# Wider column blocks for the queries and gates of a two-layer encoder: 512 columns and two token tiles to a buffer

## The chip, the cores and the metric

One core of a Trainium2 chip runs the whole program in one launch. The metric is device microseconds, first instruction to last and what lies around it, lower is better; the kernel's time is the median of several executions. The profile shown is one execution taken by the hardware profiler. The core has a matmul engine (PE, with its weight loads PEld), a vector engine (DVE), a scalar engine (ACT), a general engine (POOL) and SP, which here issues all transfers. Each takes its own instructions strictly in the order in which they were written into the program.

## The reference, cut to what matters

Two layers over 2048 tokens of 1024 features. The first is a state-space scan beside a convolution module and is untouched here. The second is sparse attention:

```
proj = rms_norm(h) @ w_in        # 1024 -> 1024 q, 1024 z, 256 k, 256 v, 512 qi, 64 ki, 8 wi
q, k, qi, ki get a partial rotary (the first 16 of each 64 columns)
score[t, s] = sum over 8 index heads of wi[t, h] * relu(qi[t, h] . ki[s])
idx = the 256 best admissible keys of each token
out = softmax(q . k[idx] / 8) @ v[idx]            # 16 heads, 4 of them on one key head
y = (out * silu(z)) @ w_out;  h + y;  final norm
```

## The kernel before, in words

Token tiles are 128 rows, 16 of them; a half is 8 tiles. In the second layer the normalised activations of one half lie transposed in SBUF, as a high and a low part (`hb`), and every projection is made of three matmuls (high by high, low by high, high by low) for each of 8 feature tiles, so that a block of columns over 8 token tiles takes 8 x 8 x 3 = 192 matmuls. `token_major` runs a block in groups of two token tiles, with three PSUM buffers (`ps_tm`); the stationary operand is a tile of `hb`, the moving one a row tile of the weights (`wh` high, `wl` low).

`load_w` fetches a block's weights in pieces of 128 x 512 numbers: a transfer into one of two staging buffers (`wst`, L106), a rounding copy on ACT (`wh`, L113) and a subtraction on POOL (`wl`, L114). There are eight buffers each for `wh` and `wl`. A block of 256 columns fills four of them, so that two blocks fit side by side.

`project_half` goes through a list of blocks. Its inner function `done` copies each finished token tile from PSUM to `ot` (two buffers; by a plain copy, or by SiLU for the gates), and when `ot` is full `finish` rotates what needs it on POOL (`rope_`, six operations) and stores it.

The order of the second layer is: both halves' index blocks (`first`), the index scores and the selection of the 256 best keys for tiles 2 to 15 (`index`), then the remaining blocks of half 1, a swap of `hb`, the remaining blocks of half 0 (`rest`: k, v, four blocks of q, four of z per half), and attention. A scheduler then merges these: it places instructions by program order as priority and by its own timeline, and what it writes is fixed for every engine. So the projections of `rest` stand between the instructions of the index work.

Index scoring goes by chunks of up to 512 keys: for each of 8 heads two matmuls into `ps_i`, a `relu` on ACT (L913) and a multiply-add on DVE (L72, into `sc` or, for the last four tiles, `scl`, which is stored to `sc_d`). There are 38 chunks; tiles 14 and 15 have the last eight. Selection (`select_mask`) searches a threshold bit by bit, 34 counting passes a tile: on DVE (L977) with two small steps on POOL (L69) behind each, or, for the odd tiles up to 13, on ACT (L994, L1002, L1004). Selection of tiles 12 to 15 is a second, late part (`late`): its first 140 steps, nearly all of tile 12, are written ahead of attention, and the rest is spread over attention by columns. Attention (`Attend`) has `ps_s` matmuls, a masked maximum on DVE (`lm`, L1121), an exponential on ACT, transposes (`ps_pt`) and values (`ps_pv`).

Of the kernel before, what the change touches and what calls it, by code (L numbers as in the profile page):

```python
# [11 lines left out]
F32 = mybir.dt.float32  # L12
# [11 lines left out]
P = 128  # L24
# [346 lines left out]
def norm_to_feature(k, tiles, layer, hT, col0, vec, ident, sm, ev, pt, split=False, parts=1):  # L371


    nc = k.nc
    n = len(tiles)
    ss = sm.tile([P, parts, n], F32, tag="ss", name="ss")
    rs = sm.tile([P, n], F32, tag="rs", name="rs")
    w = D // parts
    for i, xt in enumerate(tiles):
        junk = ev.tile([P, w], BF16, tag="junk", name="junk", bufs=1)  # L380
        for a in range(parts):
            x, acc = xt[:, a * w:a * w + w], ss[:, a, i:i + 1]
            if split and i % 2:
                nc.vector.tensor_tensor_reduce(out=junk, in0=x, in1=x, scale=1.0, scalar=0.0, op0=ALU.mult,
                                               op1=ALU.add, accum_out=acc)
            else:
                nc.scalar.activation(junk, x, AF.Square, accum_out=acc)
    for a in range(1, parts):
        k.vtt(ss[:, 0], ss[:, 0], ss[:, a], ALU.add)
    ss = ss[:, 0]  # L390
    k.vts(ss, ss, 1.0 / D, ALU.mult, EPS, ALU.add)
    k.rsqrt(rs, ss, sm, "rsq")
    for i, xt in enumerate(tiles):
        if split and i % 2:
            nc.scalar.activation(xt, xt, AF.Copy, scale=rs[:, i:i + 1])
        else:
            k.vts(xt, xt, rs[:, i:i + 1], ALU.mult)
    cols = slice(col0, col0 + n * P)
    for f in range(NF):
        ps = pt.tile([P, n, 128], F32, tag="pt", name="ps_t")  # L400
        for i, xt in enumerate(tiles):
            nc.tensor.transpose(ps[:, i], xt[:, f * P:(f + 1) * P], ident)
        g = vec[:, VEC_NG + layer * 8 + f:VEC_NG + layer * 8 + f + 1]
        hi, lo = hT[f]
        psf = ps.rearrange("p a b -> p (a b)")
        nc.scalar.activation(hi[:, cols], psf, AF.Copy, scale=g)
        k.stt(lo[:, cols], psf, g, hi[:, cols].bitcast(F32), ALU.mult, ALU.subtract)
# [7 lines left out]
def token_major(k, pj, act, W, ncol, tiles, done, group=4):  # L415


    for g in range(0, len(tiles), group):
        grp = tiles[g:g + group]
        pss = [pj.tile([P, 512], F32, tag="pj", name="ps_tm") for _ in grp]  # L420
        for f in range(NF):
            for ps, i in zip(pss, grp):
                c = slice(i * P, i * P + P)
                k.mm3(ps[:, 0:ncol], (act[f][0][:, c], act[f][1][:, c]), W[f], f == 0, f == NF - 1)
        for ps, i in zip(pss, grp):
            done(i, ps[:, 0:ncol])
# [309 lines left out]
OQ, OZ, OK, OV, OQI, OKI = 0, 1024, 2048, 2304, 2560, 3072  # L736
# [17 lines left out]
def split2(k, v, hi2, lo2):  # L754

    nc = k.nc
    for a in range(2):
        nc.scalar.copy(hi2[:, :, :, a], v)
    for a in range(2):
        nc.gpsimd.tensor_tensor(out=lo2[:, :, :, a], in0=v, in1=hi2[:, :, :, 0].bitcast(F32), op=ALU.subtract)  # L760
# [17 lines left out]
def project_half(k, h, hT, new, order, A, h1_d, S, st, rope, ident, identr, vec, pools):  # L778


    nc = k.nc
    hp, xp, ev, op, wp, sm, pj, pt = pools
    w1 = A["w_in1"]

    def rope_(t, t0, nh):

        v = t.rearrange("p t (h c) -> p t h c", c=64)
        X, Y = v[:, :, :, 0:8], v[:, :, :, 8:16]
        sh = [P, 4, nh, 8]
        c = rope[:, t0:t0 + 4, None, 0:8].to_broadcast(sh)  # L790
        s = rope[:, t0:t0 + 4, None, 8:16].to_broadcast(sh)
        r = sm.tile([P, 2, 4, 4, 8], F32, tag="ropet", name="ropet", bufs=1)
        r = r[:, :, :, 0:nh]
        g = nc.gpsimd
        k.vtt(r[:, 0], Y, s, ALU.mult, g)
        k.vtt(r[:, 1], X, s, ALU.mult, g)
        k.vtt(X, X, c, ALU.mult, g)
        k.vtt(Y, Y, c, ALU.mult, g)
        k.vtt(X, X, r[:, 0], ALU.subtract, g)
        k.vtt(Y, Y, r[:, 1], ALU.add, g)  # L800

    def both_parts(v, name):

        kd = ev.tile([P, 4, 1, 2, 64], F32R, tag="kd", name=name)
        kl = ev.tile([P, 4, 1, 2, 64], F32R, tag="kdl", name=name + "l", bufs=1)
        split2(k, v, kd, kl)
        return kd, kl

    def doubled(src, out):

        ps = pt.tile([P, 4, 128], F32R, tag="pt", name="ps_k")
        for i in range(4):
            nc.tensor.transpose(ps[:, i], src[:, i, 0].rearrange("p a b -> p (a b)"), identr)
        nc.scalar.copy(out, ps.rearrange("p a b -> p (a b)"))

    def index_key(kt, t0, rows):
        rope_(kt[:, :, 0:64], t0, 1)
        k.vts(st["wi"][:, t0:t0 + 4], kt[:, :, 64:72], float(np.float32(8 ** -0.5)), ALU.mult,
              0.125, ALU.mult, eng=nc.gpsimd)
        kd, kl = both_parts(kt[:, :, None, 0:64], "kid")  # L820
        for src, dst in ((kd, "kih"), (kl, "kil")):
            doubled(src, st[dst][:, rows])

    def stack_k(ot, rows):

        for kv in range(4):
            v = ot[:, :, None, kv * 64:kv * 64 + 64]
            kd, kl = both_parts(v, "kd")
            for src, dst in ((kd, S["kh"][kv]), (kl, S["kl"][kv])):
                ks = ev.tile([P, 512], F32R, tag="ks", name="ks", bufs=1)  # L830
                doubled(src, ks)
                nc.sync.dma_start(dst[:, rows], ks.bitcast(F32))

    for grp in range(4 if new else 0):
        with k.tc.high_priority(offset=1500):
            tiles = []
            for i in range(2):
                xt = xp.tile([P, D], F32, tag="xt", name="xt1")
                r0 = h * HALF + (grp * 2 + i) * P
                nc.sync.dma_start(xt, h1_d[r0:r0 + P])  # L840
                tiles.append(xt)
            norm_to_feature(k, tiles, 1, hT, grp * 256, vec, ident, sm, ev, pt, parts=2)

    def finish(c, ot, t0):

        rows = slice(t0 * P, t0 * P + 512)
        if c < OZ or OK <= c < OV or c >= OQI:
            rope_(ot, t0, 4)
        if c == OK:
            stack_k(ot, rows)  # L850
            return
        if c < OZ:
            dst = S["q"][rows, c:c + 256]
        elif c < OK:
            dst = S["z"][rows, c - OZ:c - OZ + 256]
        elif c == OV:
            dst = S["v"][rows]
        else:
            dst = S["qi"][rows, c - OQI:c - OQI + 256]
        nc.sync.dma_start(dst.rearrange("(t p) c -> p t c", p=P), ot)  # L860

    for c0, ncol in order:
        W = k.load_w(w1, 0, NF, c0, ncol, wp)
        cur = {}

        def done(j, ps):
            g, ji = divmod(j, 4)
            if ji == 0:
                cur["ot"] = op.tile([P, 4, 256], F32, tag="ot", name="ot")
                if ncol == 328:  # L870
                    cur["kt"] = ev.tile([P, 4, 72], F32, tag="ks", name="kit", bufs=1)
            if OZ <= c0 < OK:
                nc.scalar.activation(cur["ot"][:, ji], ps, AF.Silu)
            else:
                nc.scalar.copy(cur["ot"][:, ji], ps[:, 0:256])  # L875
            if ncol == 328:
                nc.scalar.copy(cur["kt"][:, ji], ps[:, 256:328])
            if ji == 3:
                t0 = h * 8 + g * 4
                finish(c0, cur["ot"], t0)  # L880
                if ncol == 328:
                    index_key(cur["kt"], t0, slice(t0 * P, t0 * P + 512))

        token_major(k, pj, hT, W, ncol, list(range(8)), done, 2)
# [303 lines left out]
def layer1(k, A, h1_d, S, ident, identr, vec):  # L1188
    nc, tc = k.nc, k.tc
    with ExitStack() as ctx:  # L1190
# [3 lines left out]
        with ExitStack() as c2:  # L1194
# [4 lines left out]
            wp, ev, sm = tags(junk=1, wh=8, wst=2), {}, tags(ss=2, rs=2, rsqh=2, rsqt=2)  # L1199
# [3 lines left out]
            op = pool(c2, "ot1", 2, side="right")  # L1203
            sm.update(tags(rope=1, ropet=1))
            pools = (hp, xp, Tags(ev), op, Tags(wp), Tags(sm), pool(c2, "pj1", 3, space=PSUM), pt)
            rope = pools[5].tile([P, 16, 16], F32, tag="rope", name="rope")
# [41 lines left out]
            half = lambda h, new, order: project_half(  # L1248
                k, h, hT, new, order, A, h1_d, S, st, rope, ident, identr, vec, pools)
            first = [(OKI - 256, 328), (OQI, 256)]  # L1250
            rest = [(OK, 256), (OV, 256)] + [(c + 256 * i, 256) for c in (OQ, OZ) for i in range(4)]
            half(0, True, first)
            swap_h(True)
            for i in range(2):
# [230 lines left out]
```

## Time and profile before

| what | value |
|---|---|
| median of 3 runs | 3020.63 us (3018.98 to 3023.07) |
| the profiled execution | 3015.91 us, span 3014.1 us |
| PE busy | 2753.4 us (91%), 17488 matmuls |
| DVE busy | 2072.8 us (69%) |
| ACT busy | 1733.2 us (58%) |
| POOL busy | 1105.6 us (37%) |

The profiled execution is 4.7 us below the median of the runs. Shares are averages over stages of very different kinds, so the stage that the change touches, about 1110 to 1790 us of the span, is read by itself. Matmuls are pipelined: what one takes in a stream is the distance of two starts, not the duration shown.

### The profile page before, as it was taken

To read this page: it belongs to the slowest core of one execution; us is meant where nothing else is said; L and a number is where in the kernel's file an instruction comes from. 1 tells how busy PE (TensorE), PEld (TensorE's weight loads), DVE (VectorE), ACT (ScalarE), POOL (GpSimd) and SP (SyncE) were. 2 spreads that over 40 slices of the span, in tenths; PEclk is the share of its full clock that TensorE was granted. 3 is DMA by queue.
4 is the path that set the end of the run, shared out by engine and by line. 5 is a ranking of instruction groups with operands and counts; after the bars stand their busy time and mean duration, and the time that the engine had idled before them with its cause. 6 is when DMAs were issued, how large, how long until landed. Compare 5 with 4: busy or idle time off the path is not lost. (4 is left out here: it accounts for less than half of the span.)

```text
span 3014.1 us, 47682 instructions
## 1 busy us (share of the span) xinstructions
PE 2753.4 (91%) x17488; PEld 2220.8 (74%) x17488; DVE 2072.8 (69%) x3735; ACT 1733.2 (58%) x3558; POOL 1105.6 (37%) x1517
## 2 busy tenths in 40 slices
PE   7789998799999999899889968999989999999998
PEld 5667786678999899899779946666655555666787
DVE  8899986995354556644897479734489997456444
ACT  4122332344243688888768957899965666655311
POOL 3946133732232697745774113321232121001000
PEclk9899999899999999999999979999999999999999
DMA  3254563346566323235322261111110101001332
GB/s 134 76 126 142 157 171 63 122 160 208 172 203 226 97 82 120 64 94 175 99 71 82 88 229 38 58 33 37 38 52 26 47 21 53 22 4 50 123 126 98
DMA packets 233385, 300.40 MB, mean 100 GB/s; under 512 B 14144, under 2 KB 171072, under 8 KB 233024
## 3 DMA queue, kind: packets, MB, share of 16 engines
q1 hardware_dynamic: 233152, 297.37, 31.4%
q8 instruction: 137, 2.24, 0.3%
q14 instruction: 96, 0.79, 0.1%
HBM read 194.16 MB, written 105.25 MB: 99 GB/s over the span
## 5 line engine op out<-in xcount | busy, mean ns | idle before, releaser
L114 POOL TENSOR_TENSOR wl<-wst,wh 128x512 fp32r<-128x512 f32 (+1 forms) x220 | 341.5, 1556 | 444.6 <-ACT wh L113 407.9
L121 PE MATMUL ps_tm<-wh,hb 128*128 128x256 f32 (+1 forms) x1536 | 439.3, 290 | 11.7 <-ACT ot L875 6.9
L122 PE MATMUL ps_tm<-wh,hb 128*128 128x256 f32 (+1 forms) x1536 | 444.4, 290 | 0.8 <-DVE hb L72 0.8
L123 PE MATMUL ps_tm<-wl,hb 128*128 128x256 f32 (+1 forms) x1536 | 439.9, 289 | 0.0
L1132 ACT ACTIVATE lm<-lm,mx 128x512 f32<-128x512 f32 (+15 forms) x256 | 309.1, 1209 | 135.0 <-DVE mx L1121 134.4
L1153 ACT COPY pT<-ps_pt 128x512 f32<-128x512 f32 (+1 forms) x512 | 273.6, 563 | 153.0 <-PE ps_pt L1148 127.0
L72 DVE SCALAR_TENSOR_TENSOR cvo<-hc,vec,cvo 128x1024 f32<-128x1024 f32 x240 | 356.0, 1514 | 0.8
L1121 DVE CUSTOM_DVE_ANT_0 lm<-ps_s,amb 128x1024 f32<-128x1024 f32 (+7 forms) x256 | 249.6, 985 | 152.2 <-PE ps_pt L1148 89.4
L1155 PE MATMUL ps_pv<-pT,v 128*64 128x256 f32 x2176 | 339.1, 399 | 14.6 <-DVE avt L62 8.6
L1148 PEld LDWEIGHTS ps_pt<-ident,lm 128*128 128x128 f32 x2176 | 240.1, 141 | 143.1 <-issue 125.0
L1148 PE MATMUL ps_pt<-ident,lm 128*128 128x128 f32 x2176 | 340.8, 282 | 1.8 <-ACT lm L1132 0.7
L1117 PE MATMUL ps_s<-kh,qs 128*128 128x512 f32 (+2 forms) x640 | 268.6, 421 | 48.7 <-DVE mx L1121 42.1
L121 PEld LDWEIGHTS ps_tm<-wh,hb 128*128 128x128 f32 x1536 | 296.2, 194 | 19.6 <-ACT ot L875 9.0
L69 POOL TENSOR_SCALAR sv<-sv 128x1 f32<-128x1 f32 x512 | 185.6, 363 | 321.6 <-DVE eq L977 282.9
L122 PEld LDWEIGHTS ps_tm<-wh,hb 128*128 128x128 f32 x1536 | 298.0, 194 | 6.0 <-DVE hb L72 1.5
L123 PEld LDWEIGHTS ps_tm<-wl,hb 128*128 128x128 f32 x1536 | 296.7, 194 | 4.3
L113 ACT CAST wh<-wst 128x512 fp32r<-128x512 f32 (+1 forms) x220 | 133.2, 609 | 283.2 <-DMA wst<-in_w_in 131.3
L121 PE MATMUL ps_p<-hh,wh 128*128 128x512 f32 x640 | 256.8, 404 | 18.9 <-ACT uT L520 16.5
L123 PE MATMUL ps_p<-hl,wh 128*128 128x512 f32 x640 | 256.9, 404 | 0.0
L122 PE MATMUL ps_p<-hh,wl 128*128 128x512 f32 x640 | 255.9, 400 | 0.0
L977 DVE TENSOR_SCALAR_CACHE_REDUCE eq<-klo,sv 128x384 bf16<-128x384 uint16 (+7 forms) x136 | 207.0, 1525 | 63.5 <-POOL sv L69 62.8
L977 DVE TENSOR_SCALAR_CACHE_REDUCE eq<-khi,sv 128x384 bf16<-128x384 uint16 (+7 forms) x136 | 206.8, 1525 | 48.7 <-POOL sv L69 47.4
(333 smaller groups left out, 6335.2 us busy)
## 6 DMA issues: line engine op xcount, KB each, us to landing
wst<-in_w_in SPq DMA_DIRECT2D x168, 256.0 KB, 2.9
zs_d<-zt SPq DMA_DIRECT2D x16, 512.0 KB, 3.3
zt<-zs_d SPq DMA_DIRECT2D x16, 512.0 KB, 4.4
ry<-rec_d SPq DMA_DIRECT2D x16, 512.0 KB, 4.2
xr<-in_x SPq DMA_DIRECT2D x16, 512.0 KB, 4.4
wst<-in_w_out SPq DMA_DIRECT2D x32, 256.0 KB, 3.4
h_d<-xr SPq DMA_DIRECT2D x16, 512.0 KB, 3.7
xt<-h_d SPq DMA_DIRECT2D x16, 512.0 KB, 5.7
```

The lines of the kernel that those rows point to most:

```text
L72: self.nc.vector.scalar_tensor_tensor(out=out, in0=a, scalar=s, in1=b, op0=op0, op1=op1)
L114: nc.gpsimd.tensor_tensor(out=lo, in0=st, in1=hi.bitcast(F32), op=ALU.subtract)
L121: t.matmul(ps, a[0], b[0], start=start, stop=False)
L122: t.matmul(ps, a[1], b[0], start=False, stop=False)
L123: t.matmul(ps, a[0], b[1], start=False, stop=stop)
L977: op = nc.vector.tensor_scalar(out=eq, in0=src, scalar1=u, scalar2=0.0, op0=op, op1=ALU.add, accum_out=cnt)
L1117: nc.tensor.matmul(pss[e][:, cols], qs[e][:, 2 * hp + h], src[:, e, cols], start=part == 0, stop=part == 1)
L1121: self.pace[0] = nc.vector.tensor_tensor_reduce(out=prob[e][h][:, c:c + w], in0=pss[e][:, 0:w], in1=mb[:, c:c + w], scale=-0.125, scalar=( ...
L1132: nc.scalar.activation(lm, lm, AF.Exp, bias=mxs[e, h][:, nh - 1:nh], scale=-1.0, accum_out=t["den"][:, hd:hd + 1])
L1148: nc.tensor.transpose(ps[:, s, h], prob[e][h][:, (b + s) * P:(b + s + 1) * P], ident)
L1153: nc.scalar.copy(pT[:, 0:n], ps[:, 0:n].rearrange("p s h q -> p s (h q)"))
L1155: nc.tensor.matmul(po[64 * s:64 * s + 64, e], self.kvt[(b + s) // 8, kp][2][:, (b + s) % 8, e * 64:e * 64 + 64], pT[:, s], start=b == 0, s ...
```

## The change

The blocks of q and z are made 512 columns wide, two a half instead of four. `done` then gathers two token tiles by 512 columns into an `ot` buffer where it gathered four by 256 (the same 512 KB), and `rope_` and `finish` take their sizes from the buffer. The blocks of k, v and the index stay at 256. A weight block of 512 columns fills all eight `wh` and `wl` buffers.

```diff
-        sh = [P, 4, nh, 8]
-        c = rope[:, t0:t0 + 4, None, 0:8].to_broadcast(sh)
-        s = rope[:, t0:t0 + 4, None, 8:16].to_broadcast(sh)
-        r = sm.tile([P, 2, 4, 4, 8], F32, tag="ropet", name="ropet", bufs=1)
+        nt = t.shape[1]
+        sh = [P, nt, nh, 8]
+        c = rope[:, t0:t0 + nt, None, 0:8].to_broadcast(sh)
+        s = rope[:, t0:t0 + nt, None, 8:16].to_broadcast(sh)
+        r = sm.tile([P, 2, nt, 16 // nt, 8], F32, tag="ropet", name="ropet", bufs=1)
...
-        rows = slice(t0 * P, t0 * P + 512)
+        nt, w = ot.shape[1:3]
+        rows = slice(t0 * P, (t0 + nt) * P)
         if c < OZ or OK <= c < OV or c >= OQI:
-            rope_(ot, t0, 4)
+            rope_(ot, t0, w // 64)
...
         def done(j, ps):
-            g, ji = divmod(j, 4)
+            w = 512 if ncol == 512 else 256
+            nt = 1024 // w
+            g, ji = divmod(j, nt)
             if ji == 0:
-                cur["ot"] = op.tile([P, 4, 256], F32, tag="ot", name="ot")
+                cur["ot"] = op.tile([P, nt, w], F32, tag="ot", name="ot")
...
-                nc.scalar.copy(cur["ot"][:, ji], ps[:, 0:256])
+                nc.scalar.copy(cur["ot"][:, ji], ps[:, 0:w])
...
-            if ji == 3:
-                t0 = h * 8 + g * 4
+            if ji == nt - 1:
+                t0 = h * 8 + g * nt
...
-            rest = [(OK, 256), (OV, 256)] + [(c + 256 * i, 256) for c in (OQ, OZ) for i in range(4)]
+            rest = [(OK, 256), (OV, 256)] + [(c + 512 * i, 512) for c in (OQ, OZ) for i in range(2)]
```

The scheduler orders the whole stage anew. Three places matter. The first is ACT from the last copies out of the projections to the first instructions of attention (`ot` are those copies, `relu` is index scoring, `klo` the late selection's keys, `qs` and the table load attention's). Before:

```order
L994 ACTIVATE eq,sv<-klo,sv 128x1536
L873 ACTIVATE ot<-ps_tm 128x256 x2
L913 ACTIVATE relu<-ps_i 128x512 x22
L972 COPY klo<-key 128x512 x3
L972 COPY klo<-key 128x128
```

And in the changed kernel (lines of these helpers are numbered up to four higher):

```order
L998 ACTIVATE eq,sv<-klo,sv 128x1536
L917 ACTIVATE relu<-ps_i 128x512 x3
L877 ACTIVATE ot<-ps_tm 128x512 x2
L917 ACTIVATE relu<-ps_i 128x512 x17
L917 ACTIVATE relu<-ps_i 128x384 x7
...
L917 ACTIVATE relu<-ps_i 128x384
...
L917 ACTIVATE relu<-ps_i 128x512 x2
...
L917 ACTIVATE relu<-ps_i 128x512 x30
```

Behind the last copy out of a projection stood 22 relus of index scoring; now there are 17 + 8 + 2 + 30 = 57.

The second place is DVE at the end of index scoring (`scl` is the multiply-add of a head, `eq` a counting pass of tile 12's late selection, 1664 keys wide, `lm` attention's maximum). Before:

```order
L69 TENSOR_SCALAR scl<-relu,wi 128x512
L72 SCALAR_TENSOR_TENSOR scl<-relu,wi,scl 128x512 x4
...
L971 COPY khi<-key 128x128
L977 TENSOR_SCALAR eq,sv<-khi,sv 128x1664 x3
L1121 ISA lm,mx<-ps_s,amb 128x512
```

And in the changed kernel, at the start of the third chunk from the end (the pattern of the last two rows then goes on to the end of scoring):

```order
L975 COPY khi<-key 128x512
L69 TENSOR_SCALAR key<-scr 128x512
L62 TENSOR_TENSOR key<-key,scr 128x512
L975 COPY khi<-key 128x512
L69 TENSOR_SCALAR key<-scr 128x128
L62 TENSOR_TENSOR key<-key,scr 128x128
L975 COPY khi<-key 128x128
L69 TENSOR_SCALAR scl<-relu,wi 128x512
L981 TENSOR_SCALAR eq,sv<-khi,sv 128x1664
L72 SCALAR_TENSOR_TENSOR scl<-relu,wi,scl 128x512
```

All of tile 12's counting passes stood behind scoring, three of them ahead of the first `lm`; now 23 stand between the multiply-adds of the last three chunks and two more ahead of the first `lm`, so nine of the 34 are left behind it.

The third place is SP's queue around a change of blocks in half 0 (`wst` are weight pieces, `q_d` and `z_d` stores of finished buffers). Before, a stretch of q blocks:

```order
L860 DMA q_d<-ot 128x4x256
L893 DMA qi<-qi_d 128x512
L106 DMA wst<-in_w_in 128x2x256 x3
L860 DMA q_d<-ot 128x4x256
L106 DMA wst<-in_w_in 128x2x256
L931 DMA sc_d<-scl 128x512
L860 DMA q_d<-ot 128x4x256
L106 DMA wst<-in_w_in 128x2x256 x3
```

And in the changed kernel, from the third group of a q block to the first of the next:

```order
L862 DMA q_d<-ot 128x2x512
L106 DMA wst<-in_w_in 128x512 x4
L862 DMA q_d<-ot 128x2x512
L106 DMA wst<-in_w_in 128x512 x2
L935 DMA sc_d<-scl 128x512
L1059 DMA mask_d<-eq 128x1152
L106 DMA wst<-in_w_in 128x512 x2
L862 DMA q_d<-ot 128x2x512
```

Four pieces per 256-column block were spread over the block; now the eight pieces of a block stand together between the stores of the previous block's last groups and the first store of its own.

## Rows read from the trace of the kernel before

**Rows 1.** Span and mean granted TensorE clock.
```profile
core 0: 3014.1 us, clock 0.969
```

**Rows 2.** Busy time by stretch: PE, PEld, DVE, ACT, POOL (instructions), clock, DMA, GB/s.
```profile
1300.00:1350.00 50.00, 49.81 (x395) 49.12 (x395) 22.71 (x51) 40.78 (x112) 16.46 (x22) 0.97 0.31 91
...
1500.00:1550.00 50.00, 43.80 (x310) 40.55 (x308) 47.12 (x65) 36.68 (x81) 39.27 (x68) 0.97 0.24 70
...
1650.00:1700.00 50.00, 50.00 (x389) 48.35 (x388) 30.45 (x41) 47.18 (x104) 13.76 (x10) 1.00 0.33 102
1700.00:1750.00 50.00, 49.87 (x368) 47.51 (x366) 22.73 (x40) 47.03 (x102) 0.74 (x1) 1.00 0.17 56
1750.00:1800.00 50.00, 22.34 (x64) 13.17 (x65) 38.72 (x64) 19.76 (x35) 12.46 (x18) 0.64 0.92 322
```

**Rows 3.** Timeline of PE: start, duration, instruction; last projections, first attention.
```profile
1740.50 0.39 PE L906 MATMUL ps_i<-kih,qis 128*128 128x512 f32 x1
1740.73 0.39 PE L908 MATMUL ps_i<-kil,qis 128*128 128x512 f32 x1
1740.95 0.28 PE L123 MATMUL ps_tm<-wl,hb 128*128 128x256 f32 x1
...
1743.05 0.28 PE L121 MATMUL ps_tm<-wh,hb 128*128 128x256 f32 x1
...
1744.61 0.28 PE L122 MATMUL ps_tm<-wh,hb 128*128 128x256 f32 x1
...
1748.22 0.28 PE L123 MATMUL ps_tm<-wl,hb 128*128 128x256 f32 x1
...
1790.60 0.80 PE L1117 MATMUL ps_s<-kh,qs 128*128 128x512 f32 x1 [4.85 <-ACT qs L774]
```

**Rows 4.** The tile ot: instructions with ns min/median/max.
```profile
L875 ACT COPY ot<-ps_tm x128: 350/370/409, 958.7 to 1627.7; 128x256 f32<-128x256 f32 x128
L873 ACT ACTIVATE ot<-ps_tm x64: 361/383/416, 1299.4 to 1749.6; 128x256 f32<-128x256 f32 x64
L62 POOL TENSOR_TENSOR ropet<-ot,rope x56: 448/460/929, 964.6 to 1629.7; 128x128 f32<-128x128 f32 x56
L860 SPq DMA_DIRECT2D q_d<-ot x16: 359/367/575, 1184.9 to 1633.7; - x16
```

**Rows 5.** Group of relus of 512 columns on ACT: busy us, mean ns, idle before.
```profile
L913 ACT ACTIVATE relu<-ps_i 128x512 f32<-128x512 f32 x208 | 122.7, 599 | 65.1 <-DVE sc L72 21.6 <-DVE scl L72 20.9 <-DVE scl L69 7.0
```

**Rows 6.** Timeline of ACT: tile 14's first relu, the last chunks.
```profile
1681.00 0.58 ACT L913 ACTIVATE relu<-ps_i 128x512 f32<-128x512 f32 x1
1681.48 1.57 ACT L994 ACTIVATE eq<-khi,sv 128x1536 bf16<-128x1536 uint16 x1
1682.95 0.19 ACT L994 ACTIVATION_READ_ACCUMULATOR eq<-khi,sv 128x1 f32 x1
...
1764.65 0.60 ACT L913 ACTIVATE relu<-ps_i 128x512 f32<-128x512 f32 x1 [0.39 <-DVE scl L72]
1765.50 0.60 ACT L913 ACTIVATE relu<-ps_i 128x512 f32<-128x512 f32 x1 [0.26 <-DVE scl L72]
```

**Rows 7.** Timeline of DVE: end of scoring, first counting passes, first lm.
```profile
1776.83 0.49 DVE L69 TENSOR_SCALAR scl<-relu,wi 128x512 f32<-128x512 f32 x1 [7.01 <-DMA sc_d<-scl]
...
1785.19 0.11 DVE L929 MEMSET scl<- 64x64 f32 x1
...
1790.03 1.95 DVE L977 TENSOR_SCALAR_CACHE_REDUCE eq<-khi,sv 128x1664 bf16<-128x1664 uint16 x1
1791.90 0.08 DVE L977 DVE_READ_ACCUMULATOR eq<-khi,sv 128x1 f32 x1
1792.75 1.95 DVE L977 TENSOR_SCALAR_CACHE_REDUCE eq<-khi,sv 128x1664 bf16<-128x1664 uint16 x1 [0.76 <-POOL sv L69]
...
1797.33 0.69 DVE L1121 CUSTOM_DVE_ANT_0 lm<-ps_s,amb 128x512 f32<-128x512 f32 x1
```

**Rows 8.** Weight pieces, 1110 to 1750 us: ns min/median/max, waits in us and times.
```profile
L113 ACT CAST wh<-wst x72: 603/620/648, 1122.3 to 1690.1; 128x512 fp32r<-128x512 f32 x72
...
L114 POOL TENSOR_TENSOR wl<-wst,wh x72: 1257/1294/2737, 1125.6 to 1690.8; 128x512 fp32r<-128x512 f32 x72
  ACT wh L113: 57.3, 19
  PE ps_tm L122: 13.4, 1
...
DMA to landing us min/median/max: 2.6/2.8/10.2
```

**Rows 9.** Attention by stretch, columns as in group 2.
```profile
1840.00:1890.00 50.00, 44.93 (x300) 31.58 (x299) 49.28 (x79) 35.12 (x69) 15.96 (x40) 1.00 0.10 33
...
2040.00:2090.00 50.00, 48.50 (x320) 32.25 (x318) 22.46 (x64) 47.51 (x95) 9.75 (x16) 1.00 0.12 40
...
2290.00:2340.00 50.00, 45.90 (x270) 27.32 (x270) 48.01 (x72) 28.38 (x45) 13.85 (x37) 0.97 0.05 18
...
2640.00:2690.00 50.00, 50.00 (x328) 33.56 (x327) 30.27 (x56) 26.72 (x38) 4.63 (x8) 1.00 0.02 6
```

More of the change, by code (lines that the diff above doesn't have):

```diff
@@ L852, in finish @@
         if c < OZ:
-            dst = S["q"][rows, c:c + 256]
+            dst = S["q"][rows, c:c + w]
         elif c < OK:
-            dst = S["z"][rows, c - OZ:c - OZ + 256]
+            dst = S["z"][rows, c - OZ:c - OZ + w]
         elif c == OV:
```

## The prediction

> **What bounds the kernel now.** I read the stage of the change first by the table of stretches [rows 2]. PE is full where the gates are projected (50.00 of 50 us from 1650 to 1700, 49.87 in the next 50), but so is ACT nearly (47), and from 1500 to 1550 PE has six us to spare while DVE is at 47.12. So the stage is not PE's alone: index scoring and selection run through ACT, DVE and POOL, and projections fill PE between them. The clock is at its upper level of 2.4 GHz almost throughout (0.969 over the span [rows 1]). Then the timelines around the stage's end: the last projection starts at 1748.22, attention's first matmul only at 1790.60 [rows 3]. In between tiles 14 and 15 are scored to the end on ACT and DVE (the last operation at 1785.19 [rows 7]), and PE falls to 22.34 of 50 us [rows 2]. Attention behind it has stretches of two kinds [rows 9]: where DVE counts for the late selection it is full (49.28 and 48.01) and PE is at 45 to 46; without it PE or ACT is full.
>
> The end of the stage is therefore set by the index work's last chunk, and what projections cost counts so far as they delay it.
>
> **What the edit itself costs and saves.** On PE, 16 blocks of 192 matmuls, 3072 of 256 columns, become 1536 of 512. From 1743.05 to 1744.61 thirteen steps of 256 columns took 1.56 us, 0.120 us each; two starts of 512 columns lie 0.225 apart (1740.50, 1740.73, 1740.95) [rows 3], elsewhere up to 0.23. So 368.6 us become 346 to 353, a saving of 15 to 23 us; I take 19. That the operands are projections and not scores makes no difference that a row shows. The Trainium skill (TensorE: Matmul & The Clock Gate, Back-to-back issue gap) gives a warm step as columns over 2.4 GHz plus 2.5 ns, 109.2 and 215.8 ns here. By that the edit would save 3.9 us and not 19; the 0.120 of the trace is above it, and the sum goes by the trace.
>
> On ACT 128 copies of 256 columns, 64 plain at 370 ns and 64 SiLU at 383 [rows 4], 48.2 us, become 64 of 512. None of these is in the trace; the nearest row is the relu of 512 columns out of PSUM, 599 ns [rows 5], so 38.3 us, a saving of 10 us (bounds: nothing, if each costs twice a small one, and 24 us, if it costs no more than one).
>
> POOL's rotation has 96 operations on q before and after, 128 numbers per partition each [rows 4]. Stores stay 32 of 512 KB and weight pieces 64 of 256 KB, with longer lines: no cost, covered by PE as long as the pieces come in time (below).
>
> **The new order, which weighs more.** From the two orders I counted the instructions of every engine for each scoring chunk and multiplied by the mean durations of their groups in the trace, less some 0.1 us by which ACT's and 0.07 by which DVE's overlap. For a chunk the engine with most work is taken as its time. For before this gives 382 us from the last chunk of tile 8 to tile 14's first relu (1681.00 [rows 6]), where the trace shows 392.
>
> A. Up to tile 14's first relu the changed order has 1.5 blocks more projection on PE (0.66 of a block remain instead of 2.16) and 15 more of tile 11's 34 sign passes on ACT (three remain instead of 18), each about 2.3 us (1.57 + 0.19 [rows 6] and two small steps). Against that stand the savings above. In sum PE has 8 us more there and ACT 19. Chunk by chunk the longest engine gives 15 us more; with half chunks it gives 5. I take **+10** (bounds -10, where PE's saving counts and ACT's load is hidden, and +20, ACT's).
>
> B. From there to the last scoring operation the trace shows 1681.00 to 1785.19, 104 us. DVE in the changed order has 64 multiply-adds as before, tile 11's closing steps as before, and in addition 23 counting passes of tile 12 at 2.03 us (1.95 and 0.08 [rows 7]), 47 us, and a few us of its key. While PE and ACT set this stretch before, that DVE time was free; now the first chunk beside the last projections is 18 us by PE, and DVE has 95 for the seven others: 6 and 6 for two plain ones, 11 with tile 12's keys or tile 11's end, 19, 19, 16 and 18. 113 us, and a store of scores that comes back late among attention's loads as it does at 1776.83 (7.01 us [rows 7]) makes 116 with half of it. **+12** (bounds 0, where passes only fill DVE's gaps: a scoring head takes 0.85 us, from 1764.65 to 1765.50 [rows 6], of which DVE has some 0.7; and +47, all passes added).
>
> C. From the last scoring operation to the first `lm` lie 12.1 us now (1785.19 to 1797.33), with three passes in them. Then there are two and no keys: **-7** (bounds -9 and 0).
>
> D. Attention is rid of 22 passes, 45 us of DVE, out of its first stretch. There PE gains at most what it has in a stretch without passes: 48.50 for 44.93 us of 50 [rows 9], 8% of about 140 us, 11; and the last two selections end five units earlier, so that a big unit is no longer DVE's. The same count by units gives 16 us less in all. **-14** (bounds 0 and -45).
>
> E. The weights. One block of 512 columns takes all eight buffers, so that its pieces can be converted only as the last group of the block before lets go of them. A group is 48 matmuls of 0.227, 10.9 us, a row tile of it 1.36. The next block needs its eighth piece 10.9 + 7 x 1.36 = 20.4 us after that last group begins. A piece takes 2.8 us to land, 0.37 to issue, 0.62 on ACT and 1.29 on POOL, 5.1, over two staging buffers 2.55: with two staged beforehand the eighth is ready at 1.4 + 1.9 + 6 x 2.55 = 18.6 us if nothing stands in the way. The margin is 2 us at each of six changes from one wide block to the next. Now POOL waits 57.3 us in 19 pieces for ACT's copy and once 13.4 us for PE [rows 8], so pieces do queue, 3 us at a time. Bounds 0 and six times 7 us (three pairs late by 3, less the margin), 42; since the new order puts the eight copies within about 20 us of ACT's work, just the time there is, I take **+8**. What stands behind a late copy is ACT's relus, and then scoring; behind a late subtraction POOL's steps of the selection.
>
> Sum: 10 + 12 - 7 - 14 + 8 = +9 us. Against the profiled execution's own 3015.91 that is 3025; this execution is 4.7 us below the median of the runs, so the forecast for a median is 3020.6 + 9 = **3030 us**.
>
> **The rivals.** *PE's saving comes through* (faster): PE is at 50.00 of 50 beside the gates [rows 2], so its 19 us are the stage's, the passes of B fill gaps of the scoring loop at no cost, and the attention of D keeps 14 or more. The place is the stretch where PE is full, and it decides if tile 14's first relu comes earlier than 1681. That is -19, 0, -7 and -14, with +8 for E: -32, 2989 us; against it, ACT is at 47 of 50 there as well and has 15 passes more to do by then.
>
> *Weights run dry* (slower): six changes at up to 7 us, the upper end of E, in place of 8: +43 in all, 3064 us. It decides if the first matmul of a wide block's row tiles waits on POOL. The Trainium skill (Trainium Kernel Development and Optimization, Best Practices) asks for double buffering so that transfer and work overlap; by that rule the single set of buffers here would lose. The trace's pieces queue, as said, but no run so far shows a single set.
>
> *Tail and relief cancel* (no change): B with its lower bound, A at 5 and the rest as above: 5 + 0 - 7 - 14 + 8 = -8, or with B at 12 and A at 5 +4: 3013 to 3025.
>
> **How the numbers follow.** Forecast, a small loss, 3027 to 3050: 0.35. Weights run dry, 3050 and above: 0.17. Cancelled, within 0.2% (6 us, about what a measurement of this kernel can tell from no change): 0.18. Faster, by the first rival for the most part: 0.30. The range reaches from 2990 (first rival) to 3070 (the second, with A at its upper end), with 1 in 10 left out at each end; cases of both signs hold much of the chance, and the forecast's own range is 3020 to 3050.
>
> **What would show it.** In the trace after: `ps_tm` of 512 columns 0.225 to 0.23 us apart, copies of 512 columns near 0.6 us; tile 14's first relu near 1699 (A and E), the last projection near 1714, the last scoring operation near 1815 with counting passes between the multiply-adds, the first `lm` near 1820, and from there 14 us less to the end. PE idle before `ps_tm` for POOL's `wl` would speak for the second rival; a last scoring operation at or ahead of 1785 for the first. The forecast is wrong if the order's counts do not fit the chip: if scoring in the tail goes much slower than DVE's sum, or if attention gives back all 45 us.

## The result: slower by 1.5%

The changed kernel takes 3061.47 us (median of 4 runs, 3060.58 to 3069.66), the kernel before beside it 3019.81 us (4 runs). The ratio is 1.0148, 95% interval 1.0134 to 1.0162: 42 us more. The profiled execution of the changed kernel is the longest of its four; 5.3 us of its length lie ahead of the stage (the same copy of a weight piece at the end of layer one, called the mark from here on, starts at 917.49 us before and at 922.77 after). The mark's lines, before and after:

```profile
917.49 0.62 ACT L113 CAST wh<-wst 128x512 fp32r<-128x512 f32 x1 [1.54 <-PE ps_tm L122]
```

```profile
922.77 0.62 ACT L113 CAST wh<-wst 128x512 fp32r<-128x512 f32 x1 [1.53 <-PE ps_tm L122]
```

Span and clock of the changed kernel, which answer to [rows 1], and its stretches, with columns as in [rows 2]:

```profile
core 0: 3067.9 us, clock 0.953
```

```profile
1650.00:1700.00 50.00, 48.48 (x212) 38.76 (x211) 24.51 (x34) 44.59 (x88) 11.43 (x8) 1.00 0.28 93
1700.00:1750.00 50.00, 44.47 (x185) 33.81 (x184) 25.16 (x47) 38.76 (x77) 6.81 (x6) 0.93 0.39 128
1750.00:1800.00 50.00, 24.30 (x60) 13.28 (x60) 36.74 (x55) 17.21 (x32) 7.98 (x16) 0.64 0.51 187
1800.00:1850.00 50.00, 21.67 (x45) 10.59 (x44) 43.85 (x55) 12.80 (x22) 16.19 (x29) 0.50 0.09 32
```

Before, PE was poorly filled for some 42 us between the last projection and attention [rows 3]; now for two whole stretches, 1750 to 1850, in which DVE has most to do. PE's timeline at the end of the projections, beside [rows 3]:

```profile
1734.63 0.39 PE L121 MATMUL ps_tm<-wh,hb 128*128 128x512 f32 x1
1734.86 0.40 PE L122 MATMUL ps_tm<-wh,hb 128*128 128x512 f32 x1
1735.09 0.40 PE L123 MATMUL ps_tm<-wl,hb 128*128 128x512 f32 x1
```

ACT's first relu of tile 14, beside [rows 6]:

```profile
1720.56 0.60 ACT L917 ACTIVATE relu<-ps_i 128x512 f32<-128x512 f32 x1
```

ACT's groups of copies into `ot` by shape (busy us, mean ns), beside [rows 4]:

```profile
L877 ACT ACTIVATE ot<-ps_tm 128x512 f32<-128x512 f32 x32 | 18.3, 593 | 4.1 <-PE ps_tm L123 3.9
L879 ACT COPY ot<-ps_tm 128x512 f32<-128x512 f32 x32 | 18.3, 583 | 0.0
```

POOL's subtraction of the weight pieces, 1110 to 1750 us, what it waited for and who waited for it, beside [rows 8]:

```profile
L114 POOL TENSOR_TENSOR wl<-wst,wh x72: 1262/1298/3847, 1132.0 to 1697.5; 128x512 fp32r<-128x512 f32 x72
  ACT wh L113: 58.9, 17
  PE ps_tm L122: 7.1, 1
...
  PEld ps_tm L123: 25.9, 24
  PE ps_tm L123: 17.5, 18
```

Steps of 512 columns start 0.23 us apart and copies take 0.58 to 0.59 us, as forecast. ACT's first relu of tile 14 comes at 1720.56 (forecast 1699), the last projection at 1735.09 (forecast 1714). From the mark, the last projection comes 18.4 us sooner than before (1735.09 - 922.77 = 812.3, against 1748.22 - 917.49 = 830.7), near PE's forecast saving of 19. That end is no measure of the saving alone, since the same matmuls end 35.3 us sooner with three staging buffers (table below). The last two rows above are who waited for POOL's low weights: PE, 17.5 us in 18 pieces, where before the change it waited for none.

DVE's timeline at the end of scoring, which answers to [rows 7]:

```profile
1753.36 0.49 DVE L69 TENSOR_SCALAR scl<-relu,wi 128x512 f32<-128x512 f32 x1 [3.92 <-DMA sc_d<-scl]
1753.95 5.88 DVE L72 SCALAR_TENSOR_TENSOR scl<-relu,wi,scl 128x512 f32<-128x512 f32 x7
1764.65 0.42 DVE L69 TENSOR_SCALAR scl<-relu,wi 128x384 f32<-128x384 f32 x1 [4.82 <-DMA sc_d<-scl]
...
1775.35 0.48 DVE L69 TENSOR_SCALAR scl<-relu,wi 128x512 f32<-128x512 f32 x1
1775.74 1.94 DVE L981 TENSOR_SCALAR_CACHE_REDUCE eq<-khi,sv 128x1664 bf16<-128x1664 uint16 x1
1777.61 0.08 DVE L981 DVE_READ_ACCUMULATOR eq<-khi,sv 128x1 f32 x1
1777.61 0.75 DVE L72 SCALAR_TENSOR_TENSOR scl<-relu,wi,scl 128x512 f32<-128x512 f32 x1
1778.88 1.95 DVE L981 TENSOR_SCALAR_CACHE_REDUCE eq<-khi,sv 128x1664 bf16<-128x1664 uint16 x1 [0.53 <-POOL sv L69]
1780.75 0.08 DVE L981 DVE_READ_ACCUMULATOR eq<-khi,sv 128x1 f32 x1
1780.75 0.75 DVE L72 SCALAR_TENSOR_TENSOR scl<-relu,wi,scl 128x512 f32<-128x512 f32 x1
...
1852.36 0.11 DVE L933 MEMSET scl<- 64x64 f32 x1
...
1858.95 0.69 DVE L1125 CUSTOM_DVE_ANT_0 lm<-ps_s,amb 128x512 f32<-128x512 f32 x1
```

A head without a pass takes some 0.84 us (seven in 5.88). With a pass between, multiply-adds start 3.14 us apart (1777.61, 1780.75): the multiply-add, then 0.53 us in which DVE waits for POOL's two steps that make the next threshold, then the pass. In a queue that runs in order the next multiply-add stands behind that wait. The 23 passes stand in the last four chunks, 7, 7, 5 and 4 of them, and not in the last three, as the part on the change has it; the prediction's count by chunks is the right one. The tail ends at 1852.36 (forecast 1815), the first `lm` comes at 1858.95 (forecast 1820), and from there to the end are 3067.9 - 1858.95 = 1209.0 us, where it was 3014.1 - 1797.33 = 1216.8.

### The profile page after: what moved, and what is told of

The parts are those of the page before. It is cut to its first block, busy times and chain, and to the rows that moved or that the text cites. A ratio compares the mean times of both kernels' runs of the same rounds, so it can differ in the third digit from the quotient of the medians.

```text
span 3067.9 us, 44583 instructions
## 1 busy us (share of the span) xinstructions
PE 2768.1 (90%) x15952; PEld 2145.9 (70%) x15952; DVE 2069.5 (67%) x3735; ACT 1734.7 (57%) x3494; POOL 1115.3 (36%) x1517
## 5 line engine op out<-in xcount | busy, mean ns | idle before, releaser
L121 PE MATMUL ps_tm<-wh,hb 128*128 128x512 f32 (+2 forms) x1024 | 352.4, 350 | 15.3 <-ACT ot L879 8.8
L123 PE MATMUL ps_tm<-wl,hb 128*128 128x512 f32 (+2 forms) x1024 | 348.4, 349 | 17.8 <-POOL wl L114 17.5
L122 PE MATMUL ps_tm<-wh,hb 128*128 128x512 f32 (+2 forms) x1024 | 355.9, 349 | 0.8 <-DVE hb L72 0.8
L1159 PE MATMUL ps_pv<-pT,v 128*64 128x256 f32 x2176 | 344.0, 402 | 12.5 <-DVE avt L62 10.1
L69 POOL TENSOR_SCALAR sv<-sv 128x1 f32<-128x1 f32 x512 | 195.1, 382 | 346.4 <-DVE eq L981 306.8
L917 ACT ACTIVATE relu<-ps_i 128x512 f32<-128x512 f32 (+3 forms) x304 | 162.6, 544 | 135.2 <-DVE scl L72 79.0
L1121 PE MATMUL ps_s<-kl,qs 128*128 128x512 f32 (+2 forms) x640 | 234.9, 372 | 0.0
L123 PEld LDWEIGHTS ps_tm<-wl,hb 128*128 128x128 f32 x1024 | 196.2, 193 | 45.9 <-POOL wl L114 25.9
```

Source lines behind the costliest of these rows:

```text
L121: t.matmul(ps, a[0], b[0], start=start, stop=False)
L122: t.matmul(ps, a[1], b[0], start=False, stop=False)
L123: t.matmul(ps, a[0], b[1], start=False, stop=stop)
L1121: nc.tensor.matmul(pss[e][:, cols], qs[e][:, 2 * hp + h], src[:, e, cols], start=part == 0, stop=part == 1)
L1159: nc.tensor.matmul(po[64 * s:64 * s + 64, e], self.kvt[(b + s) // 8, kp][2][:, (b + s) % 8, e * 64:e * 64 + 64], pT[:, s], start=b == 0, s ...
```

## The experiments

Theory 1 is the forecast's main cause, the passes in the tail; theory 2 its second rival, the single set of weights. Medians of the runs; the ratios are to the kernel before on the same chip.

**Passes held behind scoring.** One issue order is added; the change itself stays.

```diff
-            nc.vector.memset(o[0:64, w - 64:w], NEG)
+            k.scored = nc.vector.memset(o[0:64, w - 64:w], NEG)
...
-            done, pace = set(range(LATE)), [None]
+            done, pace = set(range(LATE)), [k.scored]
```

> The changed kernel with one issue order added: tile 12's counting passes may not stand ahead of the last operation of index scoring on DVE. Every engine's order up to the tail stays as in the changed kernel; nothing is left out. Theory 1 (passes in the tail): in the changed kernel a scoring head with a pass takes 3.15 us (start to start on DVE) and one without 0.85, so 23 passes cost 23 x 2.3 = 53 us there; they go back into attention, whose part from the first lm on is 1209 us with them done and 1217 us in the kernel before, and the gap to the first lm grows from 6.5 to 12. Net -53 + 8 + 5 = -40 us: 3021 us, last scoring operation near 1800. Theory 2 (weights run dry): the loss lies in the projections ahead of the tail, the passes fill DVE's idle time: -10 us at most, 3051 us or more.

Measured 3025.96 us, 1.0023 (1.0006 to 1.0039). DVE's timeline from the same place on:

```profile
1775.89 0.48 DVE L69 TENSOR_SCALAR scl<-relu,wi 128x512 f32<-128x512 f32 x1
1776.40 5.88 DVE L72 SCALAR_TENSOR_TENSOR scl<-relu,wi,scl 128x512 f32<-128x512 f32 x7
1782.20 0.48 DVE L69 TENSOR_SCALAR scl<-relu,wi 128x512 f32<-128x512 f32 x1
...
1802.19 0.11 DVE L933 MEMSET scl<- 64x64 f32 x1
...
1810.03 0.69 DVE L1125 CUSTOM_DVE_ANT_0 lm<-ps_s,amb 128x512 f32<-128x512 f32 x1
```

The last four chunks take 26.3 us (1775.89 to 1802.19) in place of 77.0 (1775.35 to 1852.36): 50.7 us for 23 passes, 2.2 each. Of that some 35 come through to the median. Theory 1 stands for most of the loss. What is left of it is that, although PE's saving is there, the kernel isn't faster than before.

**The same passes put into the kernel before.** Blocks stay at 256.

```diff
+        self.heads, self.passes = [], 0
...
-                        k.stt(o, r, wv, o, ALU.mult, ALU.add)
+                        k.heads.append(k.stt(o, r, wv, o, ALU.mult, ALU.add))
...
+        if i == LATE and k.passes < 23:
+            k.after(k.heads[k.passes - 24], op)
+            k.passes += 1
```

> The kernel before, blocks of 256 columns, with the suspected loss put into it: 23 counting passes of tile 12 are ordered, one by one, ahead of the last 24 multiply-adds of index scoring, as the changed kernel's order has them. The order up to the tail stays that of before, and nothing is left out. Theory 1 (a pass in the tail costs 2.3 us, whatever the width of the blocks): +53 us to the last scoring operation, 5 less to the first lm, 8 less in attention: +40 us, 3050 to 3068 us. Theory 2 (the passes only fill DVE's gaps where PE or ACT sets the tail): +10 us at most, 3015 to 3030 us.

Measured 3082.4 us, 1.0214 (1.0188 to 1.024): more than expected. Rows of DVE's timeline:

```profile
1787.14 0.43 DVE L70 TENSOR_SCALAR key<-scr 128x512 int32<-128x512 int32 x1 [21.24 <-DMA scr<-sc_d]
...
1795.37 0.75 DVE L73 SCALAR_TENSOR_TENSOR scl<-relu,wi,scl 128x512 f32<-128x512 f32 x1
...
1798.52 0.75 DVE L73 SCALAR_TENSOR_TENSOR scl<-relu,wi,scl 128x512 f32<-128x512 f32 x1
...
1868.74 0.11 DVE L930 MEMSET scl<- 64x64 f32 x1
```

And one of SP's:

```profile
1782.81 0.32 SPq L1287 DMA_DIRECT2D scr<-sc_d  x1
```

The heads take 3.15 us each again (1795.37 to 1798.52). In addition DVE waits 21.24 us for tile 12's scores, since their load stands in SP's queue behind loads of attention and is issued only at 1782.81. From tile 14's first relu (1689.44) to the last scoring operation are 179.3 us instead of 104.2; 23 x 2.3 + 21.2 = 74 of the 75 are these two. The width of the blocks has no part in the price of a pass.

**One part alone.** The list of blocks holds q in 512 and the gates in 256, or the other way round.

```diff
-            rest = [(OK, 256), (OV, 256)] + [(c + 512 * i, 512) for c in (OQ, OZ) for i in range(2)]
+            rest = [(OK, 256), (OV, 256)] + [(OQ + 512 * i, 512) for i in range(2)] + [(OZ + 256 * i, 256) for i in range(4)]
```

> Only q in blocks of 512, the gates in blocks of 256 as before. In the order that results no pass of tile 12 stands ahead of the last scoring operation, and 26 relus stand behind the last projection copy (22 before, 57 with the change). Theory 1: half of PE's saving (9 us), no loss in the tail, some weights waits: 3005 to 3022 us. Theory 2: two changes wide to wide and two wide to narrow instead of six, so about half of the loss: 3035 to 3050 us.

> Only the gates in blocks of 512, q in blocks of 256. In the order that results 18 passes of tile 12 stand ahead of the last scoring operation, and 51 relus behind the last projection copy. Theory 1: 18 x 2.3 = 41 us in the tail, 10 given back in attention, 9 saved on PE: 3035 to 3050 us, at least 20 us above the run with q alone. Theory 2: the same number of wide blocks as with q alone, so within 10 us of that run, 3035 to 3050 us both.

Measured 3032.81 us (1.0049, 1.003 to 1.0068) and 3057.03 us (1.014, 1.0118 to 1.0162). The one with passes in its tail is 24 us above the other, as theory 1 asks; both lie above its ranges, so that it misses a loss of some 10 us that is there without passes too. Nor does q alone show its half of PE's saving: its projections end 3.9 us later than before (table below). Theory 2's equal loss isn't there.

**More buffers for the weights.** With the passes held, ten buffers for high and low weights, paid for with two of the four buffers for the rows to be normalised; and those two taken away alone.

```diff
-            xp = pool(c2, "xp1", 4, side="right")
+            xp = pool(c2, "xp1", 2, side="right")
...
-            wp, ev, sm = tags(junk=1, wh=8, wst=2), {}, tags(ss=2, rs=2, rsqh=2, rsqt=2)
+            wp, ev, sm = tags(junk=1, wh=10, wst=2), {}, tags(ss=2, rs=2, rsqh=2, rsqt=2)
...
-            wp.update(tags(wl=8))
+            wp.update(tags(wl=10))
```

> As the run with the issue order, and ten instead of eight buffers each for the high and low weights, for which the buffers of the rows to be normalised go from four to two. Theory 2 (weights run dry): PE's 43 us of waits for POOL's low weights shrink by half or more, and 15 to 30 us come off against the run with eight buffers: 2990 to 3005 us if that one is at 3021. Theory 1: PE's waits for weights are short gaps in which ACT and DVE go on with scoring; within 8 us of the run with eight buffers, 3013 to 3029 us.

> The run with ten weight buffers without the ten buffers: tile 12's passes held, eight weight buffers, and only two buffers for the rows to be normalised. If these two missing buffers made the run with ten slow (later tiles of the second half, another order), this one is at 3045 us or above; if the ten buffers did it, it is near the first run, 3021 to 3031 us.

Measured 3061.13 us (1.0147, 1.0125 to 1.0168) and 3051.42 us (1.0104, 1.0085 to 1.0124). The pair is no test of the weights: the two buffers taken away cost 25 us by themselves, and PE waits 4.7 us for POOL's low weights without the ten buffers (1110 to 1740 us) and 4.3 with them.

**Three staging buffers.** Paid for with one of two buffers of key pairs; that one alone, and both in the kernel before, are the controls.

```diff
-        kd = ev.tile([P, 4, 1, 2, 64], F32R, tag="kd", name=name)
+        kd = ev.tile([P, 4, 1, 2, 64], F32R, tag="kd", name=name, bufs=1)
...
-        W = k.load_w(w1, 0, NF, c0, ncol, wp)
+        W = k.load_w(w1, 0, NF, c0, ncol, wp, 3)
...
-            wp, ev, sm = tags(junk=1, wh=8, wst=2), {}, tags(ss=2, rs=2, rsqh=2, rsqt=2)
+            wp, ev, sm = tags(junk=1, wh=8, wst=3), {}, tags(ss=2, rs=2, rsqh=2, rsqt=2)
...
-            ev.update(tags(kdl=1, kd=2, ks=1))
+            ev.update(tags(kdl=1, kd=1, ks=1))
```

> As the first run (tile 12's passes held behind scoring), with three instead of two staging buffers for weight pieces, for which the buffer of key pairs goes from two to one. The order of the tail stays (63 relus behind the last projection copy instead of 57). In the first run PE waits 19.0 us in 19 pieces for POOL's low weights between 1110 and 1860 us. Theory 2, now for what is left of the loss: the piece's way from transfer to subtraction over two staging buffers is too slow for a single set; with three the waits fall under 8 us and the kernel is 10 to 20 us below the first run, 3006 to 3016 us. Theory 1: PE is not alone the bound there, the waits are gaps that scoring has to spare: within 5 us of the first run, 3021 to 3031 us.

> Control to the run with three staging buffers: only the buffer of key pairs goes from two to one, with tile 12's passes held. Both theories: within 5 us of the first run, 3021 to 3031 us. If it is above by more, what three staging buffers bring is to be read against this one.

> Control: the kernel before with three staging buffers and one buffer of key pairs. Its PE does not wait for POOL's low weights in the stage, so under both theories it stays within 6 us of the kernel before, 3012 to 3024 us. If it gains as much as the held kernel does, the gain isn't that of the single set of weights.

Measured 3012.55 us (0.9985, 0.9975 to 0.9996), 3026.24 us (1.0031, 1.0014 to 1.0047) and 3017.87 us (0.9994, 0.9982 to 1.0007). Against its control the third staging buffer brings 13.7 us to the wide blocks, and nothing to the narrow ones. It is the only version that beats both kernels, and that by 0.15%, less than I called measurable. The time is the one that theory 2 forecast, but not by its way. PE's waits for POOL's low weights, 1110 to 1740 us, fall to 9.7 us and not under 8, and the control, which is no faster than the first run, has 12.5 already (three staging buffers first, then one key buffer alone):

```profile
PE ps_tm L123 <- POOL wl L114: 9.7, 11, 2.5
```

```profile
PE ps_tm L123 <- POOL wl L114: 12.5, 12, 2.7
```

**Low weights left out, one set and two.** POOL's subtraction goes into the staging buffer, the third matmul reads `wh`.

```diff
-                    lo = wp.tile([P, n, ncol], F32R, tag="wl", name="wl")
+                    lo = hi if same else wp.tile([P, n, ncol], F32R, tag="wl", name="wl")
...
-                nc.gpsimd.tensor_tensor(out=lo, in0=st, in1=hi.bitcast(F32), op=ALU.subtract)
+                nc.gpsimd.tensor_tensor(out=st if same else lo, in0=st, in1=hi.bitcast(F32), op=ALU.subtract)
...
-        W = k.load_w(w1, 0, NF, c0, ncol, wp)
+        W = k.load_w(w1, 0, NF, c0, ncol, wp, same=True)
...
-            wp.update(tags(wl=8))
```

> As the first run (tile 12's passes held), but what POOL subtracts is written back to the staging buffer and the third matmul reads the high weights in place of the low ones: the low part of these weights is left out, with the same matmuls, copies, transfers and POOL steps. PE then waits for ACT's copy alone. Theory 2 for what is left (the single set's refill, POOL's step last in it, costs 13 us): 3008 to 3018 us, and no wait of PE for POOL's weights. Rival (three staging buffers helped by the order that they brought, not by the waits): within 5 us of the first run, 3021 to 3031 us.

> As the run without the low weights, with sixteen instead of eight buffers for the high weights, in the room that the low ones leave: two whole sets of 512 columns side by side. Theory 2: what a single set still costs goes too, so 0 to 10 us below the run with eight, 3000 to 3015 us. Rival: no difference to the run with eight beyond 5 us, since refilling a set is quick enough once POOL isn't in the way.

Measured 3028.88 us (1.0027, 1.0008 to 1.0047) and 3021.53 us (1.0021, 1.0006 to 1.0035). The first lies in the rival's range: with no wait for POOL's weights nothing is gained. The second is 7.4 us below the first, which is what theory 2 asks and more than the rival's 5, though it is above theory 2's 3015 and the intervals of the two ratios overlap. What PE waited for between 1110 and 1740 us: first with passes held (the first run), then with sixteen buffers, of which PE waits for no weights worth a row.

```profile
PE ps_tm L123 <- POOL wl L114: 19.0, 19, 3.1
```

```profile
PE ps_i L910 <- ACT relu L917: 33.2, 25, 4.5
```

With eight buffers PE still waits 11.2 us for ACT's copies, in 9 pieces. Between 1110 and 1700 us the wait for relus was 15.7 us in the first run and is 29.0 with sixteen buffers, the same as before the change (29.3), and PE is busy for 528.1 us in the first run and 531.8 with sixteen. By these rows the waits for weights had taken the place of waits for scoring. Against the run with passes held the time differs by 4.4 us, within the two intervals. So what PE is seen to wait for weights is mostly not what the kernel loses by them.

**Gates alone, passes held, three staging buffers.** The issue order, the third staging buffer with one key buffer, and the list of the second run of *one part alone*.

> Only the gates in blocks of 512, tile 12's passes held and three staging buffers. Half of PE's saving, 9 us, and half of the changes of a wide set. If PE's saving counts once tail and weights are mended: midway between the kernel before with three staging buffers (3018) and the whole change mended (3012.5), 3010 to 3020 us. If the order of the stage weighs more than the width: outside of that.

Measured 3024.46 us, 1.0025 (1.0008 to 1.0042), outside the range for "PE's saving counts". The last scoring operation comes 868.7 us after the mark, as in the kernel before (867.7); the loss is in attention, 1227.6 us from the first `lm` on.

**All runs side by side**, from their timelines, in us (those with two buffers less for the rows to be normalised and those without low weights left out). Relus: those behind the last copy out of a projection in the order of ACT. Tail: from the last `ps_tm` to the last scoring operation.

| kernel | relus | passes in the tail | mark to last projection | tail | first `lm` to end |
|---|---|---|---|---|---|
| before | 22 | 0 | 830.7 | 37.0 | 1216.8 |
| before, three staging | 22 | 0 | 828.2 | 36.8 | 1221.2 |
| q alone | 26 | 0 | 834.6 | 42.5 | 1225.5 |
| gates alone, held, three staging | 46 | 0 | 810.5 | 58.2 | 1227.6 |
| held | 57 | 0 | 809.1 | 67.2 | 1218.5 |
| held, one key buffer | 57 | 0 | 808.1 | 67.3 | 1223.7 |
| held, three staging | 63 | 0 | 795.4 | 72.2 | 1216.7 |
| gates alone | 51 | 18 | 815.0 | 101.0 | 1208.7 |
| changed | 57 | 23 | 812.3 | 117.3 | 1209.0 |
| before with passes | 25 | 23 | 830.2 | 112.0 | 1205.7 |

Without passes the tail goes by the relus left: from 22 to 63 it grows by 35.2 us, 0.86 for each, the time of a head. No run changed the number of relus alone, so this is read from the table and not shown by an experiment. With the passes held the projections end 21.6 us sooner than before, the tail is 30.2 longer. With three staging buffers they end 35.3 us sooner and the tail is 35.2 longer, so that the last scoring operation comes 867.6 us after the mark, where it came 867.7 before: projections that end earlier have not ended the index work earlier. What that version gains in its trace lies between the last scoring operation and the first `lm`, 7.9 us (1785.56 to 1793.41) in place of 12.1.

## Why the prediction was right in sign and 31 us short

*The edit itself* was right in the main: 0.23 us a step, copies of 0.58 to 0.59. At 0.23 the 1536 steps take 353 us and the saving is 15 us, the lower end of 15 to 23 and not the 19 that I took; that the projections end 18.4 us sooner is the new order's work too, and its nearness to 19 is luck. The Trainium skill (TensorE: Matmul & The Clock Gate, Back-to-back issue gap) gives 215.8 ns for that step by its formula, which it calls the gap of an isolated matmul, and some 131 ns for a stream of them. The trace agrees with neither: the step is 0.23 us here, and the saving is there because the narrow step takes 0.120 us [rows 3] and not the 109 ns of the formula. The estimate of the saving by that formula is 3.8 us and not 3.9.

*C and D* were right in sign: C -5.5 (12.1 to 6.6) for -7; D -7.8 for -14, about half. The run with passes put into the kernel before gives back 11.1 in attention.

*The passes in B* were right in mechanism and nearly in size: forecast were 19 + 19 + 16 + 18 = 72 us for the last four chunks, measured 77.0. The step that takes 2.03 us of DVE for a pass missed that its trip over POOL stands in the queue too; 2.2 to 2.3 is the price.

*A, E and the front of B* were the terms that were mis-sized. A and E together were +18 up to tile 14's first relu (forecast 1699); it came at 1720.56, 34 us later by the mark. B was +12 and is 131.8 - 104.2 = +27.6, of which the first four chunks made 54.8 us (1720.56 to 1775.35) where I had 41 and half of a late store: they hold 5.5 us of DVE's waits for relus, tile 11's closing steps, and 8.7 us of waits for two late stores. Together +62 in place of +30. What failed is the split at tile 14's first relu and the pricing chunk by chunk by the busiest engine. Seen from the last projection the matter is simpler. PE's saving brings that forward, and every head left behind it then costs 0.85 us with PE partly idle: 35 heads more, 30 us, more than the 21.6 by which the projections end sooner with the passes held. With the passes held, my own terms would have given a gain of some 16 us (+9, less 46 for the passes, 72 against 26 us in the last four chunks, plus the 21 of C and D given back); the kernel lost 0.23%, 7 us.

*E* by itself: the sign that I named, PE idle before `ps_tm` for POOL's weights, did appear (17.5 us). It doesn't prove *weights run dry*, whose 3064 us is near the result by another way: two whole sets take the waits out and 4.4 us off, 7.4 against one set without the low weights, where that rival priced the six changes at 42. So the range up to 3070, which was drawn from that rival, holds the result by luck; the forecast's own range, 3020 to 3050, does not. The Trainium skill's rule cited for that rival (Trainium Kernel Development and Optimization, Best Practices) is to double-buffer, so that transfers overlap with work. It is borne out only weakly here by a second set, by those 4 to 7 us; a third staging buffer gave 13.7 us. Why that one gives more than a second set stays open: ACT's waits for staged pieces (1110 to 1740 us) fall from 23.3 us in its control to 8.8 with it, against 17.5 with sixteen buffers, and ACT's relus stand behind them, but no run changed this alone.

*PE's saving comes through* failed at the point that I gave for it, tile 14's first relu: it came at 1720.56, not ahead of 1681. What also stays open is why attention, with the same passes left to it, takes between 1216.7 and 1227.6 us in these kernels.

## What to carry to other kernels

Where projections fill an engine beside a chain of small dependent steps, count the steps that an order leaves behind the last projection, and price each at the chain's own pace; making the projections shorter can lengthen that tail by as much as it saves, or more. A pass written between the links of such a chain costs its length and its round trip over the other engine. A wait seen on the busiest engine is worth what remains when it is removed, and here most of it moved to the next operand.

## What the runs showed of the hardware

- In the tail of the changed kernel the granted clock is 0.50 (1800 to 1850 us), the 1.2 GHz level, after a stretch in which PE was busy for 24.30 of 50 us; no cost of it shows, since DVE sets the pace of the heads (43.85 of 50 us busy): seven heads without a pass take the same 5.88 us at a mean granted clock of 0.76 (changed kernel, 1753 to 1760 us) and of 0.96 (passes held, 1776 to 1802 us).
- An ACT copy of 512 columns out of PSUM takes 0.583 us plain and 0.593 with SiLU, against 0.370 and 0.383 for 256 columns [rows 4]: over a fifth less for the same data.
- The place in SP's queue outweighs the transfer: DVE waited 21.24 us for tile 12's scores, of which only 4.3 lie behind the load's issue (1782.81 to 1787.14).
